# A hybrid S5 and pooling layer on one core: identity transposes at the start, the first projection ahead of the third tile, halves for the first loads, two queues for the last stores

## The chip, the cores and the metric

The kernel runs on one core of a Trainium2 chip (trn2). The metric is the device time of one execution in microseconds. TensorE is called PE here, VectorE DVE, ScalarE ACT, GpSimd POOL and SyncE SP.

## The reference, cut to what matters

One decoder layer: 2048 prompt tokens and 8 sample tokens, 1024 wide, all in float32.

```python
proj = h @ w_in                                  # (2048 + 8, 1024) @ (1024, 2048)
s_in, s_gate, p_in, p_gate = split(proj)         # four parts, 512 wide
sy, hr, hi = s5_mixer(s_in, ...)                 # 32 groups of 16 channels, complex state of 64, scan over time
sy = gelu(sy); sy = sy * sigmoid(sy @ glu_w + glu_b)
py, buf = pool_mixer(p_in, ...)                  # trailing means over 2, 4, 8, 16 tokens, a map per group
mixed = concatenate([sy * silu(s_gate), py * silu(p_gate)])
y = layer_norm(DN_ALPHA * h + mixed @ w_out)
```

## The kernel before, in words

**Precision.** Products run in the fp32r format, with each operand split in a high part (ACT converts, line 155) and a low part (DVE or POOL subtracts, line 149). A product of two operands is three matmuls: high by high, and the two mixed ones. `split` (line 154) does one tile.

**Start.** `load_x(i)` (line 497) loads tile i of the input, 128 tokens by 1024 (512 KB), `put_x(i)` (line 513) transposes it in eight 128x128 steps on PE against the constant `ident` (tile name pt, line 146), and splits the result into xh and xl. There are 16 prompt tiles and one of 8 sample tokens. `load_w` and `split_w` (lines 173, 179) load and split a 128-column piece of w_in (tiles wst and w). `proj(m, c)` (line 195) multiplies piece m by a chunk c of tokens, 8 blocks of k by 3 split terms = 24 matmuls into a PSUM bank pj; the first two chunks have 256 columns, then 512. `u_tile` (line 524) copies pj to ue on ACT and stores it as u_d. The first four m are the input of the S5 mixer.

**Parameters.** Between these, `params` (line 221) makes the tables of the S5 mixer from lambda, log_dt, B and C: small operations on DVE, a few transposes on PE (ps_par, which read nat; ps_c), 16 small copies prv on ACT (line 346), bbar on DVE, and then, per pair of groups, products on POOL (bd, qp, qq), sp on DVE, and ps_ks on PE (lines 428 and 146). `tables` (line 460) makes rotation tables (tb) on DVE.

**Middle and end.** 16 pairs of groups go through the scan (`ssm_task`): the input ut is split into uh, PE multiplies (s, line 629), ACT copies to SP, DVE turns and scans, PE multiplies by the output maps (y, pm). Projections for the gates and the pooling branch fill PE in between, each with a weight split w on ACT and DVE. Then come the GLU, the output projection and the layer norm; `out_last` (line 1132) ends the last tile of 128 tokens in two column halves, each stored in two pieces by `ln_store` (line 1071).

**What sets the order.** PE, ACT, DVE and POOL run their instructions in the order in which the program issues them. A clock by hand sets this order: `Line` (line 46) holds a time `line.t`, which `proj` moves on by 3n/2400 for every three matmuls and `put_x` by 0.9, and a list of generator tasks with due times; a task gives its next due time with `yield`. `line.t = 0.0` is set at line 550, after the first tiles. SP's queue, which issues all DMAs, is ordered by a scheduler of the framework. The buffers of the input tiles (xst two, xw two halves) are reused every four tiles, and a DMA waits also for the earlier one whose semaphore it takes, of eight.

Of the kernel before, what the change touches and what calls it, by code (L numbers as in the profile page):

```python
# [17 lines left out]
P = 128  # L18
# [3 lines left out]
KT = 8  # L22
# [20 lines left out]
HL = ((0, 0), (0, 1), (1, 0))  # L43
# [58 lines left out]
def hybrid_step(  # L102
# [9 lines left out]
    xp, xs = x_prompt[0], x_sample.rearrange("b l d -> (b l) d")  # L112
    wi, wo = w_in[0], w_out[0]
    dma = nc.sync.dma_start
    V, S, G = nc.vector, nc.scalar, nc.gpsimd
    line = Line()
# [5 lines left out]
    wst = ctx.enter_context(tc.tile_pool(name="wstage", bufs=1))  # L122
# [5 lines left out]
    def bank(name):  # L128
        return mm.tile([P, 512], F32, tag="bank", name=name)

    def pair(name):
        return pr.tile([P, 2, 512], F32, tag="pair", name=name)
# [12 lines left out]
    def transpose(out, in_, n):  # L145
        nc.tensor.transpose(out, in_, ident[:n, :n])
# [4 lines left out]
    def sub_hi(src, hi, lo, eng=None):  # L151
        tt(lo, src, hi.bitcast(F32), ALU.subtract, eng)

    def split(src, hi, lo, eng=None):
        S.copy(out=hi, in_=src)  # L155
        sub_hi(src, hi, lo, eng)
# [10 lines left out]
    def xcols(a, k, t0, n):  # L167
        h = t0 // 1024
        return xT[a][h][:, k, t0 - 1024 * h:t0 - 1024 * h + n]

    wtiles, wpend, ready, shared = {}, {}, {}, {}

    def load_w(src, key, pool=None, tag="wst"):
        st = (pool or wst).tile([P, KT * P], F32, tag=tag, name=f"wst_{key}")
        k = src.shape[0] // P
        dma(out=st.rearrange("p (k c) -> p k c", k=k), in_=src.rearrange("(k p) c -> p k c", p=P))
        return st

    def split_w(st, key, eng=None):
        w = wpool.tile([P, 2, KT * P], F32R, tag="w", name=f"w_{key}")  # L180
        split(st, w[:, 0], w[:, 1], eng)
        wtiles[key] = w

    def w_task(src, key, delay=4.0):
# [6 lines left out]
    def w_in_task(m, delay=6.4):  # L191
        wpend[m] = w_task(wi[:, P * m:P * m + P], m, delay)
        return wpend[m]

    def proj(m, c):
        t0, n, s = c
        n += s
        if m in wpend:
            line.finish(wpend.pop(m))
        ps = bank(f"pj{m}_{t0}")  # L200
        w = wtiles[m].rearrange("p a (k c) -> p a k c", k=KT)
        if m < 2:
            order = [(k, a, b) for a, b in ((0, 0), (1, 0), (0, 1)) for k in range(KT)]
        else:
            order = [(k, 0, b) for k in range(KT) for b in range(2)] + [(k, 1, 0) for k in range(KT)]
        for i, (k, a, b) in enumerate(order):
            nc.tensor.matmul(out=ps[:, :n], lhsT=w[:, a, k], rhs=xcols(b, k, t0, n), start=(i == 0), stop=(i == 23))  # L207
            if i % 3 == 2:
                line.go(3 * n / 2400.0)
        return ps  # L210

    ident = const.tile([P, P], F32, name="ident")
# [247 lines left out]
    def tables():  # L460
        while "table" not in ready or "x" not in ready:
            yield 0.5
        zs = shared["zs"]
        for q in range(4):
            tb = tabs[0].tile([P, 2, 4, HC], F32, tag="tb", name=f"tb{q}")
            V.memset(tb[:, 0, :, 0:1], 1.0)
            V.memset(tb[:, 1, :, 0:1], 0.0)
            for lv in range(6):
                n = 2 ** lv
                mt = tabs[0].tile([P, 2, 2, 128], F32, tag="mt", name="mt")  # L470
                mv = [mt[:, i, :, :4 * n].rearrange("p a (g c) -> p a g c", g=4) for i in range(2)]
                cmul(tb[:, :, :, n:2 * n], tb[:, :, :, 0:n],
                     [zs[:, c, 1 + lv, 4 * q:4 * q + 4].unsqueeze(1).unsqueeze(3) for c in range(2)],
                     mv[0], mv[1], [P, 2, 4, n])
                yield (1.12, 0.8, 0.8, 1.0, 1.4, 2.2)[lv]
            for a in range(2):
                dma(out=tb_d[4 * q:4 * q + 4, :, a].rearrange("g p c -> p g c"), in_=tb[:, a])
            yield 7.0
# [18 lines left out]
    def load_x(i):  # L497
        if i == 2:
            xstage["w"] = wpool.tile([P, 2, D], F32, tag="w", name="xw")
        if i % 4 > 1:  # L500
            st = xstage["w"][:, i % 2]
        else:
            st = xst.tile([P, D], F32, tag="x", name=f"xst{i}")
        if i == 0:
            for h in range(2):
                dma(out=st[:, 512 * h:512 * h + 512], in_=xp[0:P, 512 * h:512 * h + 512])
        elif i < 16:
            dma(out=st, in_=xp[P * i:P * i + P, :])
        else:
            dma(out=st[:NB], in_=xs)  # L510
        xstage[i] = st

    def put_x(i):
        st, n = xstage.pop(i), P if i < 16 else NB
        ps = pair(f"pt{i}")
        pv = ps.rearrange("p a b -> p (a b)").rearrange("p (k t) -> p k t", k=KT)
        for k in range(KT):
            transpose(pv[:, k, :n], st[:n, P * k:P * k + P], n)
        line.t += 0.9
        h, c = (i // 8, P * (i % 8)) if i < 16 else (1, 1024)  # L520
        hi, lo = (xT[a][h][:, :, c:c + n] for a in range(2))
        split(pv[:, :, :n], hi, lo)

    def u_tile(m, c):
        t0, n, s = c
        ps = proj(m, c)
        k0, nk = t0 // T, n // T
        ue = ga.tile([P, T, 64], F32, tag="g", name=f"ue{m}_{t0}")
        uv = ue.rearrange("p j k -> p (j k)")[:, :n].rearrange("p (j k) -> p j k", j=T)
        S.copy(out=uv, in_=ps[:, :n].rearrange("p (k j) -> p j k", j=T))  # L530
        dma(out=u_d[:, P * m:P * m + P, k0:k0 + nk].rearrange("j c k -> c j k"), in_=uv)
        if s:
            S.copy(out=us[:, m], in_=ps[:, n:n + s])

    PD = 0.5
    load_x(0)
    load_x(1)
    st0 = load_w(wi[:, 0:P], 0)
    load_x(2)
    load_x(3)  # L540
    st1 = load_w(wi[:, P:2 * P], 1, prod, "hl")
    put_x(0)
    load_x(4)
    split_w(st0, 0)
    put_x(1)
    load_x(5)
    put_x(2)
    load_x(6)
    split_w(st1, 1, G)
    line.t = 0.0  # L550
    par = line.add(params(ptmp, prod), PD)
    tab = line.add(tables(), 10.0)

    def x_task():
        for i in range(3, 17):
            put_x(i)
            if i + 4 < 17:
                load_x(i + 4)
            done.append(i)
            yield 2.88  # L560
        rx.close()
        with tc.using_default_side("right"):
            tabs.append(rx.enter_context(tc.tile_pool(name="tabs", bufs=1)))
        ready["x"] = True

    done = [2]
    xg = line.add(x_task(), 0.38)

    def need_x(i):
        while not done or done[-1] < i:  # L570
            for x in line.tasks:
                if x[1] is xg:
                    line.step(x)
                    break

    for c in CHUNKS_U:
        last = min(16, (c[0] + c[1] + P - 1) // P - 1) if not c[2] else 16
        if last > 1:
            need_x(last)
        for m in range(2):  # L580
            u_tile(m, c)
        if c[0] == 512:
            line.add(w_in_task(2))
# [484 lines left out]
    def ln_shift(mv, n):  # L1068
        V.scalar_tensor_tensor(out=mv[:n, 0:1], in0=mv[:n, 0:1], scalar=-1.0, in1=mv[:n, 2:3], op0=ALU.mult, op1=ALU.mult)  # L1069

    def ln_store(yout, ot, n, c):
        for j in range(len(yout)):
            dma(out=yout[j][:, c], in_=ot[j * n // len(yout):(j + 1) * n // len(yout), c])

    def ln_tail(xt, st, n, yout, nm):
        mv = ln_scale(st, n, nm)
# [55 lines left out]
    def out_last(mix, c0, xin, yout, nm):  # L1132
        xt = out_load(xin, P, nm)
        st = xo.tile([P, 3, 6], F32, tag="ste", name="ste", bufs=1)
        for i, (h, c) in enumerate(((0, full), (1, slice(0, 256)), (1, slice(256, 512)))):
            ps = po.tile([P, 512], F32, tag="o", name=f"o{nm}_{i}")
            out_mm(ps[:, c], lambda a, k: mix[:, a, k, c0:c0 + P], h, c, HL)
            ln_part(xt, ps[:, c], st[:, i], P, slice(512 * h + c.start, 512 * h + c.stop))
        mv = ln_scale(st, P, nm)
        cs = [slice(512 * h, 512 * h + 512) for h in range(2)]  # L1140
        for c in cs:
            V.scalar_tensor_tensor(out=xt[:, c], in0=xt[:, c], scalar=mv[:, 0:1], in1=gb[:, 0, c], op0=ALU.subtract, op1=ALU.mult)
        for c in cs:
            V.scalar_tensor_tensor(out=xt[:, c], in0=xt[:, c], scalar=mv[:, 2:3], in1=gb[:, 1, c], op0=ALU.mult, op1=ALU.add)
            ln_store(yout, xt, P, c)

    xpv = xp.rearrange("(k j) d -> j k d", j=T)
    ypv = y_prompt[0].rearrange("(k j) d -> j k d", j=T)
# [17 lines left out]
    for ck, (t0, n, s) in enumerate(CHUNKS[i] for i in BO):  # L1166
# [10 lines left out]
        for i in range(nt):  # L1177
            xin, yout = ([v[j, k0:k0 + nk, :] for j in range(nj * i, nj * i + nj)] for v in (xpv, ypv))
# [42 lines left out]
```

## Time and profile before

| what | value |
|---|---|
| three timed runs | 713.64, 714.81 (median), 717.47 us |
| the profiled execution, its own time | 712.72 us |
| span of the profile | 710.9 us |
| mean granted clock of TensorE | 0.987 |
| busy: PE, DVE, ACT, POOL | 96%, 70%, 33%, 27% of the span |

The span runs from the first instruction to the last; the execution's own time is 1.8 us longer. PE's busy time counts a matmul from its start to a modelled end, so 96% busy is not 96% of what PE could do.

### The profile page before, as it was taken

Reading aid. Unit: us, or ns where it says so; the run is one execution under the profiler, and the core shown is the slowest. Engines: PE = TensorE matmul, PEld = TensorE weight load, DVE = VectorE, ACT = ScalarE, POOL = GpSimd, SP = SyncE. Lnnn points to the kernel's source line nnn. Section 1 sums busy time; section 2 is a strip of 40 time slices with the busy share of each in tenths; the row PEclk is TensorE's granted clock in tenths of the full one; section 3 lists DMA queues with packets and bytes.
Section 4 is the critical chain, followed back from the end, with each engine's and each line's share of the span. In section 5 each row is a group of like instructions: output and inputs, shape, how many; then the busy total and the mean of one; then the engine's idle time right before and its main releaser. Section 6 shows DMA issues by size and latency. Waiting matters only on the chain.

```text
span 710.9 us, 10871 instructions
## 1 busy us (share of the span) xinstructions
PE 682.5 (96%) x3735; PEld 578.5 (81%) x3735; DVE 497.5 (70%) x1129; ACT 232.7 (33%) x471; POOL 195.5 (27%) x250
## 2 busy tenths in 40 slices
PE   6999899999999999999998999989999999999995
PEld 5988787888888888888977887777888868888884
DVE  3689889652679798888988893686555647647444
ACT  4343223331344344443332332353321332323100
POOL 1005444400000121232133213664314333062222
PEclk9999999999999999999998999999999999999998
DMA  8993578666555443443434326945454662633432
GB/s 275 226 336 112 141 208 204 190 211 184 161 164 160 131 138 110 141 123 101 138 116 122 94 90 140 356 131 114 115 117 124 142 155 62 148 105 103 118 90 59
DMA packets 133686, 105.86 MB, mean 149 GB/s; under 512 B 70211, under 2 KB 111335, under 8 KB 133623
## 3 DMA queue, kind: packets, MB, share of 16 engines
q1 hardware_dynamic: 133631, 105.17, 52.5%
q8 instruction: 29, 0.48, 0.3%
q14 instruction: 26, 0.21, 0.1%
HBM read 63.69 MB, written 41.68 MB: 148 GB/s over the span
## 4 chain that ended last, share of the span: by engine, by line
PE 63%; DVE 12%; ACT 3%; POOL 2%; DMA 2%; issue 2%; SPq 1%; DVEq 0%; ACTq 0%; POOLq 0%
PE pj L207 28%; PE o L1090 24%; PE z L1050 5%; POOL ws L149 2%; DVE SP L149 2%; DVE B L718 1%; PE y L644 1%; PE s L629 1%; PE os L1090 1%; PE y L702 1%; ACT SP L682 1%; PE pm L854 1%; DVE B L149 1%; DVE ini L714 1%; DVE w L149 1%
## 5 line engine op out<-in xcount | busy, mean ns | idle before, releaser
L207 PE MATMUL pj<-xh,w 128*128 128x512 f32 (+2 forms) x1312 | 336.1, 349 | 0.0
L207 PEld LDWEIGHTS pj<-xh,w 128*128 128x128 f32 x1312 | 226.0, 191 | 30.0
L207 PE MATMUL pj<-xl,w 128*128 128x512 f32 (+2 forms) x656 | 207.3, 348 | 0.0
L1090 PE MATMUL o<-wo,mix 128*128 128x512 f32 (+1 forms) x792 | 176.1, 383 | 0.8 <-ACT mix L155 0.8
L1090 PEld LDWEIGHTS o<-wo,mix 128*128 128x128 f32 x792 | 145.2, 188 | 30.7 <-ACT mix L155 1.1
L207 PEld LDWEIGHTS pj<-xl,w 128*128 128x128 f32 x656 | 120.3, 190 | 14.9
L149 POOL TENSOR_TENSOR xr<-xr,gb 128x1024 f32<-128x1024 f32 x15 | 36.0, 2398 | 48.4 <-DVE xr L149 43.1
L688 POOL COPY bus<-SP 128x16 f32<-128x16 f32 x16 | 9.3, 582 | 137.6 <-ACT SP L682 137.6
L1050 PE MATMUL z<-yh,w_g 128*128 128x512 f32 (+2 forms) x240 | 47.0, 356 | 0.0
L149 POOL TENSOR_TENSOR ws<-pc 128x527 f32<-128x527 f32 (+1 forms) x20 | 21.9, 1096 | 91.0 <-ACT pc L805 39.6
L1050 PEld LDWEIGHTS z<-yh,w_g 128*128 128x128 f32 x240 | 39.9, 193 | 6.7
L1079 ACT ACTIVATE xr<-xr,mv 128x1024 f32<-128x1024 f32 x15 | 18.7, 1244 | 79.4 <-DVE mv L1069 79.4
L1058 DVE SCALAR_TENSOR_TENSOR xr<-xr,o 128x512 f32<-128x512 f32 (+1 forms) x33 | 22.0, 667 | 26.1 <-PE o L1090 26.1
L149 POOL TENSOR_TENSOR ws<-ws 128x525 f32<-128x525 f32 (+5 forms) x30 | 37.6, 1252 | 3.3 <-DVE dh L149 1.1
L149 DVE TENSOR_TENSOR xl<-pt,xh 128x1024 fp32r<-128x1024 f32 (+1 forms) x17 | 19.8, 1164 | 17.4 <-ACT xh L155 17.3
L149 POOL TENSOR_TENSOR mv<-mv,mhalf 128x1 f32<-128x1 f32 x16 | 9.9, 618 | 74.5 <-DVE mv L1064 74.5
L718 DVE TENSOR_TENSOR_SCAN B<-r,ini,SP 128x64 f32<-128x64 f32 x96 | 29.8, 354 | 0.0
L149 DVE TENSOR_TENSOR yh<-y,yh 128x512 fp32r<-128x512 f32 (+2 forms) x20 | 12.2, 610 | 21.7 <-ACT yh L155 21.7
L149 DVE TENSOR_TENSOR mix<-y,mix 128x512 fp32r<-128x512 f32 (+2 forms) x20 | 18.3, 914 | 12.0 <-ACT mix L155 12.0
L155 ACT CAST hh<-hf 128x528 fp32r<-128x528 f32 x16 | 10.1, 633 | 50.2 <-DVE hf L149 47.3
L149 DVE TENSOR_TENSOR xr<-xr,gb 128x1024 f32<-128x1024 f32 x15 | 18.3, 1220 | 10.5 <-ACT xr L1079 10.5
L682 ACT COPY SP<-s 64x264 f32<-64x264 f32 x64 | 23.8, 372 | 3.8 <-PE s L629 3.2
(218 smaller groups left out, 881.1 us busy)
## 6 DMA issues: line engine op xcount, KB each, us to landing
wst<-in_w_in_dram SPq DMA_DIRECT2D x16, 512.0 KB
xr<-in_x_prompt_dram SPq DMA_DIRECT2D x24, 256.0 KB
out_dram<-xr SPq DMA_DIRECT2D x22, 256.0 KB
xw<-in_x_prompt_dram SPq DMA_DIRECT2D x8, 512.0 KB
wt_d<-wzero SPq DMA_DIRECT2D x4, 1024.0 KB
sw_d<-sv SPq DMA_DIRECT2D x8, 512.0 KB
qw_d<-qh SPq DMA_DIRECT2D x16, 256.0 KB
ws<-sw_d SPq DMA_DIRECT2D x16, 256.0 KB
```

Of the source, the lines that this page charges most:

```text
L149: (eng or V).tensor_tensor(out=out, in0=a, in1=b, op=op)
L155: S.copy(out=hi, in_=src)
L207: nc.tensor.matmul(out=ps[:, :n], lhsT=w[:, a, k], rhs=xcols(b, k, t0, n), start=(i == 0), stop=(i == 23))
L629: nc.tensor.matmul(out=ps[:, c, 0:264], lhsT=ws[:, c, a], rhs=uh[:, b, c, 8:272], start=(i == 0), stop=(i == 2))
L644: nc.tensor.matmul(out=py[:, c, 0:264], lhsT=wq[cs, r, a], rhs=hh[cs, b, r], start=False, stop=(i == 5))
L682: S.copy(out=SP[64 * c:64 * c + 64, a], in_=ps[64 * a:64 * a + 64, c, 0:264])
L688: G.tensor_copy(out=bus[:, :, :, gp], in_=SP[:, :, 256:264])
L718: V.tensor_tensor_scan(out=B4[:, a, h], data0=dec, data1=A4[:, a, h], initial=ini[a], op0=ALU.mult, op1=ALU.add)
L1050: nc.tensor.matmul(out=ps[:, :n], lhsT=w[:, a, k, P * (m % 2):P * (m % 2) + P], rhs=yh[:, b, k, :n], start=(i == 0), stop=(i == 11))
L1058: V.scalar_tensor_tensor(out=xt[:n, c], in0=xt[:n, c], scalar=ALPHA, in1=ps, op0=ALU.mult, op1=ALU.add)
L1079: S.activation(out=xt[:n], in_=xt[:n], func=AF.Identity, scale=mv[:n, 2:3], bias=mv[:n, 0:1])
L1090: nc.tensor.matmul(out=ps, lhsT=lhs(a, k), rhs=wo_view(k)[:, b, 512 * h + c.start:512 * h + c.stop], start=(i == 0), stop=(i == len(hl) * ...
```

## The change

It has seven parts.

1. After the first loads are issued, `busy(12)` puts 12 transposes of the constant `ident` on PE; 8 more follow after tile 0 and 8 after tile 1. Nothing reads their result.
2. Tile 1 and weight 0 are loaded in two halves, as tile 0 was; tiles 0 and 1 and weight 0 are split in two halves.
3. Tile 2 is no longer transposed ahead of the first projection. It is the first step of the task that brings the other tiles, due at 0.8 and then 1.1 later; the next steps are 2.88 apart as before.
4. The first chunk's projections take the split terms in another order: high weight by high and low input, then the low weight.
5. The split of weight 1 stands just ahead of the second projection.
6. `line.t = 0.0` is set before tile 2's transposes and not after them.
7. In `out_last` the stores of the first column half go out on ACT's queue.

```diff
-    def load_w(src, key, pool=None, tag="wst"):
+    def load_w(src, key, pool=None, tag="wst", parts=1):
...
-        dma(out=st.rearrange("p (k c) -> p k c", k=k), in_=src.rearrange("(k p) c -> p k c", p=P))
+        kp = k // parts
+        for i in range(0, k, kp):
+            dma(out=st.rearrange("p (k c) -> p k c", k=k)[:, i:i + kp], in_=src[P * i:P * (i + kp)].rearrange("(k p) c -> p k c", p=P))
...
-        split(st, w[:, 0], w[:, 1], eng)
+        n = KT * P // parts
+        for i in range(0, KT * P, n):
+            split(st[:, i:i + n], w[:, 0, i:i + n], w[:, 1, i:i + n], eng)
...
-            order = [(k, a, b) for a, b in ((0, 0), (1, 0), (0, 1)) for k in range(KT)]
+            order = [(k, a, b) for a, b in (HL if t0 == 0 else ((0, 0), (1, 0), (0, 1))) for k in range(KT)]
...
-        if i == 0:
+        if i < 2:
             for h in range(2):
-                dma(out=st[:, 512 * h:512 * h + 512], in_=xp[0:P, 512 * h:512 * h + 512])
+                dma(out=st[:, 512 * h:512 * h + 512], in_=xp[P * i:P * i + P, 512 * h:512 * h + 512])
...
-        split(pv[:, :, :n], hi, lo)
+        if i < 2:
+            for k in range(0, KT, 4):
+                split(pv[:, k:k + 4, :n], hi[:, k:k + 4], lo[:, k:k + 4])
+        else:
+            split(pv[:, :, :n], hi, lo)
...
+    def busy(n):
+
+        ps = pair("busy")
+        for i in range(n):
+            transpose(ps[:, i % 2, 0:P], ident, P)
+
...
-    st0 = load_w(wi[:, 0:P], 0)
+    st0 = load_w(wi[:, 0:P], 0, parts=2)
...
+    busy(12)
     put_x(0)
     load_x(4)
-    split_w(st0, 0)
+    busy(8)
     put_x(1)
     load_x(5)
-    put_x(2)
-    load_x(6)
-    split_w(st1, 1, G)
+    busy(8)
+    split_w(st0, 0, parts=2)
     line.t = 0.0
...
-        for i in range(3, 17):
+        for i in range(2, 17):
...
-            yield 2.88
+            yield 2.88 if i > 2 else 1.1
...
-    done = [2]
-    xg = line.add(x_task(), 0.38)
+    done = [1]
+    xg = line.add(x_task(), 0.8)
...
         for m in range(2):
+            if m and c[0] == 0:
+                split_w(st1, 1, G)
             u_tile(m, c)
...
-    def ln_store(yout, ot, n, c):
+    def ln_store(yout, ot, n, c, q=dma):
         for j in range(len(yout)):
-            dma(out=yout[j][:, c], in_=ot[j * n // len(yout):(j + 1) * n // len(yout), c])
+            q(out=yout[j][:, c], in_=ot[j * n // len(yout):(j + 1) * n // len(yout), c])
...
-            ln_store(yout, xt, P, c)
+            ln_store(yout, xt, P, c, dma if c.start else S.dma_start)
```

The start of PE's program before (pt: transposes of a tile, pj: a projection; each row is one kind of instruction and its count):

```order
L146 MATMUL pt_127<-ident,xst_115 128x128 x8
L146 MATMUL pt_143<-ident,xst_118 128x128 x8
L146 MATMUL pt_156<-ident,xw 128x128 x8
L207 MATMUL pj_0_171<-xh_85,w_140 128x256 x6
L146 MATMUL pt_178<-ident,xw 128x128 x8
L207 MATMUL pj_0_171<-xh_85,w_140 128x256 x10
L207 MATMUL pj_0_171<-xl_87,w_140 128x256 x8
```

And with the change, up to the parameter transposes:

```order
L146 MATMUL busy<-ident 128x128 x12
L146 MATMUL pt_142<-ident,xst_115 128x128 x8
L146 MATMUL busy<-ident 128x128 x8
L146 MATMUL pt_166<-ident,xst_118 128x128 x8
L146 MATMUL busy<-ident 128x128 x8
L211 MATMUL pj_0_195<-xh_85,w_190 128x256 x8
L211 MATMUL pj_0_195<-xl_87,w_190 128x256
L146 MATMUL pt_215<-ident,xw 128x128 x8
...
L211 MATMUL pj_0_260<-xh_85,w_257 128x256 x6
L146 MATMUL pt_267<-ident,xst_155 128x128 x8
L211 MATMUL pj_0_260<-xh_85,w_257 128x256 x2
L211 MATMUL pj_0_260<-xl_87,w_257 128x256 x8
L211 MATMUL pj_0_260<-xh_85,w_257 128x256 x5
L146 MATMUL ps_par<-ident,nat 128x16 x3
```

Tile 2 (pt_215) has moved behind nine matmuls of the first projection, and the parameter transposes ps_par from behind tile 5 to inside the second projection, ahead of it.

ACT's program, the conversions of the first tiles and weights with the change (xh: a tile, w: a weight, ue: the copy of a projection):

```order
L155 CAST xh_85<-pt_142 128x4x128 x2
L155 CAST xh_85<-pt_166 128x4x128 x2
L155 CAST w_190<-wst_121 128x512 x2
L155 CAST xh_85<-pt_215 128x8x128
L155 CAST xh_85<-pt_230 128x8x128
L538 COPY ue_0_254<-pj_0_195 128x256
L155 CAST w_257<-wst_127 128x1024
```

Weight 1 (w_257) stands behind the copy ue of the first projection; before, it stood behind tile 2. Further on, at the last full tiles, ACT's program before and then with the change (xh_86 from pt_666, then from pt_745, is tile 15):

```order
L155 CAST xh_86<-pt_606 128x8x128
L329 COPY cc<-ps_c 64x256 x4
L155 CAST xh_86<-pt_666 128x8x128
L346 COPY prv_677<-pw 128x16 x8
L346 COPY prv_678<-pw 128x16 x8
L155 CAST w_726<-wst_594 128x1024
```

```order
L155 CAST xh_86<-pt_648 128x8x128
L333 COPY cc<-ps_c 64x256 x4
L350 COPY prv_705<-pw 128x16 x8
L350 COPY prv_706<-pw 128x16 x8
L155 CAST xh_86<-pt_745 128x8x128
L155 CAST w_756<-wst_622 128x1024
```

Tile 15 has moved from ahead of the 16 copies prv to behind them.

DVE's program in the middle, at the fourteenth of the 16 pairs of groups, before and then with the change (B and ini: the scan, dh: the pooling branch, w: the low part of a weight, uh: the low part of the next pair's input):

```order
L149 TENSOR_TENSOR dh_0_4322<-df_0_4318,dh_0_4322 128x512
L712 TENSOR_SCALAR ini_3_4328<-B_4228,z_96 128x2
L714 SCALAR_TENSOR_TENSOR ini_3_4328<-B_4228,z_96,ini_3_4328 128x1 x2
L718 SCALAR_TENSOR_TENSOR B_4228<-r_94,ini_3_4328,SP_4223 128x64 x2
L149 TENSOR_TENSOR w_4340<-wst_4247,w_4340 128x1024
L149 TENSOR_TENSOR uh_4356<-ut,uh_4356 128x544
L149 TENSOR_TENSOR SP_4223<-B_4228,tbl_4124 128x2x256
```

```order
L149 TENSOR_TENSOR dh_0_4370<-df_0_4366,dh_0_4370 128x512
L149 TENSOR_TENSOR uh_4376<-ut,uh_4376 128x544
L149 TENSOR_TENSOR SP_4256<-B_4261,tbl_4129 128x2x256
L149 TENSOR_TENSOR B_4261<-B_4261,tbl_4129 128x512
L149 TENSOR_TENSOR hf<-SP_4256,B_4261 128x256 x2
L149 TENSOR_TENSOR w_4400<-wst_4305,w_4400 128x1024
L149 TENSOR_TENSOR hh_4412<-hf,hh_4412 128x528
```

The weight's low part has moved from ahead of uh to behind hf.

## Rows read from the trace of the kernel before

**Rows 1.** The page: busy time of each engine, share of the span, instructions.
```profile
PE 682.5 (96%) x3735; PEld 578.5 (81%) x3735; DVE 497.5 (70%) x1129; ACT 232.7 (33%) x471; POOL 195.5 (27%) x250
```
**Rows 2.** PE's waits over the run: for whom, us in total, times, longest.
```profile
PE s L629 <- DVE uh L149: 3.6, 2, 2.8
PE ps_ks L146 <- DVE sp L149: 3.5, 2, 2.7
PE pm L854 <- ACT dh L155: 3.4, 3, 1.4
```
**Rows 3.** Timeline, PE at the head: start, duration, instruction, count [idle before].
```profile
7.87 1.97 PE L146 MATMUL pt<-ident,xst 128*128 128x128 f32 x8 [1.71 <-DMA xst<-in_x_prompt_dram]
...
11.02 1.94 PE L146 MATMUL pt<-ident,xw 128*128 128x128 f32 x8 [1.18 <-DMA xw<-in_x_prompt_dram]
...
12.61 1.63 PE L207 MATMUL pj<-xh,w 128*128 128x256 f32 x6
...
14.04 1.91 PE L146 MATMUL pt<-ident,xw 128*128 128x128 f32 x8
...
18.18 1.04 PE L146 MATMUL pt<-ident,xst 128*128 128x128 f32 x8
```
**Rows 4.** Timeline, PE from the third chunk's approach to its second tile.
```profile
23.25 1.70 PE L207 MATMUL pj<-xh,w 128*128 128x256 f32 x12
...
24.80 1.04 PE L146 MATMUL pt<-ident,xw 128*128 128x128 f32 x8
...
30.84 0.87 PE L207 MATMUL pj<-xh,w 128*128 128x512 f32 x3
...
31.54 1.04 PE L146 MATMUL pt<-ident,xst 128*128 128x128 f32 x8
```
**Rows 5.** Timeline, ACT and DVE at the head.
```profile
9.56 1.04 ACT L155 CAST w<-wst 128x1024 fp32r<-128x1024 f32 x1 [2.35 <-DMA wst<-in_w_in_dram]
...
20.16 0.38 ACT L530 COPY ue<-pj 128x256 f32<-128x256 f32 x1
...
21.45 0.20 DVE L242 COPY nat<-dt 16x128 f32<-16x128 f32 x1
```
**Rows 6.** Timeline, tile 15 and the first ps_ks.
```profile
55.87 2.04 ACT L346 COPY prv<-pw 128x16 f32<-128x16 f32 x16 [0.65 <-DVE pw L149]
55.88 1.22 DVE L149 TENSOR_TENSOR xl<-pt,xh 128x1024 fp32r<-128x1024 f32 x1
...
59.09 1.30 DVE L149 TENSOR_TENSOR bm<-bbar,q 128x512 f32<-128x512 f32 x2
...
73.88 1.19 PE L146 MATMUL ps_ks<-ident,sp 128*128 128x128 f32 x4 [2.67 <-DVE sp L149]
```
**Rows 7.** Timeline, DVE's kv and a later ps_ks on PE.
```profile
80.38 0.41 DVE L149 TENSOR_TENSOR kv<-kf,kv 32x256 fp32r<-32x256 f32 x1 [2.27 <-ACT kv L155]
...
110.31 0.92 PE L146 MATMUL ps_ks<-ident,sp 128*128 128x128 f32 x4 [0.79 <-DVE sp L149]
```
**Rows 8.** Timeline, the fourteenth pair of groups.
```profile
371.77 2.04 DVE L149 TENSOR_TENSOR w<-wst,w 128x1024 fp32r<-128x1024 f32 x1
...
373.73 1.58 DVE L149 TENSOR_TENSOR uh<-ut,uh 128x544 fp32r<-128x544 f32 x1
...
375.37 1.47 PE L629 MATMUL s<-uh,ws 128*128 128x264 f32 x5 [2.85 <-DVE uh L149]
```
**Rows 9.** Stretches: length, busy PE, PEld, DVE, ACT, POOL, then PEclk, DMA share, GB/s.
```profile
320.00:330.00 10.00, 9.24 (x45) 7.48 (x44) 9.00 (x25) 1.62 (x5) 2.13 (x2) 1.00 0.32 103
375.00:382.00 7.00, 6.63 (x19) 5.48 (x20) 5.34 (x9) 3.22 (x8) 1.55 (x3) 0.53 0.54 158
```
**Rows 10.** Timeline, the end: DVE's last operations and SP's last four stores.
```profile
705.17 1.41 DVE L1144 SCALAR_TENSOR_TENSOR xr<-xr,mv,gb 128x512 f32<-128x512 f32 x2
705.95 2.39 SPq L1073 DMA_DIRECT2D out_dram<-xr  x4
```
**Rows 11.** Timeline, SP: issue of the first two cn loads.
```profile
21.62 3.04 SPq L240 DMA_DIRECT2D cn<-in_ssm_c_re_dram  x2
```

More of the change, by code (lines that the diff above doesn't have):

```diff
@@ L171, in hybrid_step, with split_w @@
     wtiles, wpend, ready, shared = {}, {}, {}, {}
-    def load_w(src, key, pool=None, tag="wst"):
+    def load_w(src, key, pool=None, tag="wst", parts=1):
         st = (pool or wst).tile([P, KT * P], F32, tag=tag, name=f"wst_{key}")
         k = src.shape[0] // P
-        dma(out=st.rearrange("p (k c) -> p k c", k=k), in_=src.rearrange("(k p) c -> p k c", p=P))
+        kp = k // parts
+        for i in range(0, k, kp):
+            dma(out=st.rearrange("p (k c) -> p k c", k=k)[:, i:i + kp], in_=src[P * i:P * (i + kp)].rearrange("(k p) c -> p k c", p=P))
         return st
-    def split_w(st, key, eng=None):
+    def split_w(st, key, eng=None, parts=1):
         w = wpool.tile([P, 2, KT * P], F32R, tag="w", name=f"w_{key}")
-        split(st, w[:, 0], w[:, 1], eng)
+        n = KT * P // parts
+        for i in range(0, KT * P, n):
+            split(st[:, i:i + n], w[:, 0, i:i + n], w[:, 1, i:i + n], eng)
         wtiles[key] = w
```

## The prediction

> **What bounds the kernel now.** I read the page first, then the list of waits, then the timeline at the places that the diff touches. TensorE is busy for 96% of the span [rows 1], so a gain elsewhere counts only where PE waits. The list of waits says where that is: at the head, at one transposition behind DVE (ps_ks), and in the middle behind uh and dh [rows 2]. At the head PE waits for tile 0, for tile 1 (1.71 us before 7.87) and for tile 2 (1.18 us before 11.02). The 8 transposes at 7.87 and 11.02 take 1.97 and 1.94 us, at 18.18 they take 1.04 [rows 3]: the granted clock is printed as 1.00 for both, but the durations fit the lower level (1.2 GHz) and the full one (2.4 GHz). From 11.02 on it has no wait of half a microsecond until 71.2.
>
> **The head.** Now 28 identity transposes fill PE's waits from about 1.4 us on (12 by 0.243, from 1.94/8, end at 4.3; tile 0's transposes then start later and cost nothing, since tile 1 lands at 7.87 anyway). I take it that they bring the full rate by about 7 us. Then tile 1 is transposed at 7.9 to 8.4, ACT converts its second half by 9.0 and the first half of weight 0 by 9.7 (half of the 1.04 us of [rows 5]); the first product starts at 9.7 where it started at 12.61 behind tile 2. From [rows 4], 12 products take 1.55 us (24.80 - 23.25), 0.129 each, and the 48 products and two tiles from 23.25 to 30.84 take 7.59, so a tile's 8 transposes step PE by 0.7. So: 9 products to 10.9, tile 2 (landed 11.0) to 11.8, 3 products to 12.2, tile 3 (landed between 11.0 and 14.0; I take 12.6) to 13.4, 12 products to 14.9, last result 15.1.
>
> Here a new wait comes: the split of weight 1 now stands behind the copy ue on ACT (the order shows it), and ue needs the last product. 0.38 for ue and 1.04 for the conversion [rows 5] plus hand-overs: the second projection starts at 16.65, PE idle 1.5. POOL's low half (about 2.4, twice DVE's 1.22 for the size [rows 6], an estimate) is needed 2.9 us after that and is in time. A second wait follows: PE reaches the parameter transposes after 6 products, tile 4 and 15 products, at 20.1, but they need the copy nat, which DVE does behind tile 4's low half: from the start of tile 4's transposes to the end of nat it took 3.47 us (18.18 to 21.65, [rows 3, 5]), so 17.4 + 3.47 = 20.9. With 0.5 for those transposes (an estimate, five at about 0.1) and then 51 products and three tiles (7.59 + 0.4 + 0.7), the 512-column chunk starts at **30.1 instead of 30.84**: 0.7 gained of the 2.9 at the start.
>
> SP: three more DMA issues lie in front of the second weight, and since each queue slot waits for its last load, tiles 4 and 5 are issued behind weight 0 and tile 3, and tiles 6 and 7 behind bbar and three cn loads, two of which took 3.04 us to issue [rows 11]. That puts tiles 6 and 7 at some 19 us, and PE wants them at 24.7 and 27.6. I cost it at nothing; it hides behind the products in between, and is worth up to 1.5 us where those loads take over 5 us.
>
> **To 75 us.** The table of tiles is now three 512-column products later in PE's order: tile 8 comes at 30.1 + 6 x 0.233 = 31.5, where it came at 31.54 [rows 4]. So DVE gets each tile when it got it, and the 0.7 us is no gain to DVE, which is full from 43 us on and for which PE waits 2.67 us at 73.88 [rows 6]. One thing is worse. ACT now converts tile 15 behind the 16 small prv copies. DVE is done with pw at 55.87; the copies take 2.04, the conversion 1.0: 58.9. DVE has 2.0 us of q work ahead of it (57.10 to 59.09 in [rows 6]), now from 55.9 to 57.9, then waits 1.0 us for tile 15. All behind it is later by that, so PE resumes at 74.9 instead of 73.88. POOL's products come later too, by 1.0 and the weight split of 1.2 that DVE now does ahead of bbar; PE needs them just ahead of the same stall, where DVE is later still. And three products that PE had done ahead of the stall are now behind it, 0.4 us: **+1.4** in all, the head's gain swallowed by a longer stall. If the wait for tile 15 is hidden it is +0.4; if tiles 6 and 7 are late as well, up to +2.9.
>
> **To 115 us.** The u_d stores now leave SP ahead of the table stores that they waited behind, so ACT's ue and kv come earlier and DVE's 2.27 us wait for kv goes; the sp products also stand ahead of six table operations. DVE is then ahead, and the wait of 0.79 us at 110.31 goes [rows 7]: **-0.8** (between 0 and -0.8).
>
> **The middle.** Line time now holds 0.9 us more at the same product, so every later task stands some three products earlier in PE's order, and pieces on DVE trade places. One trade lies on a wait. Before, the split of a weight stood ahead of uh at the fourteenth group: w 2.04, uh 1.58, and PE waited 2.85 us for uh, right behind another 0.8 [rows 2, 8]. The clock then fell: granted 0.53 on the mean of 375 to 382, which loses 7 x 0.47 = 3.3 us of full-rate work; waits of up to 1.4 us [rows 2] left it at 1.00 in 320 to 330 [rows 9]. Now uh stands ahead of w. That can save the 2.0 of w and, with the idle time down from 3.7 to about 1.7, 3 of the slow stretch. But DVE's work is the same by the next group, and it is 90% busy there [rows 9]: part of it will be asked back. I take **-2.5**, half of 2.0 + 3.0; the ends are -6.7 (3.7 idle and 3.0) and +1.0 (a w's 2.0 us put in front of another wait, half hidden).
>
> **The end.** Four stores issue on SP in 2.39 us from 705.95, 0.6 each, and DVE is done at 706.58 [rows 10]. With the first two on ACT's queue, SP issues the last two from 706.6, so the last leaves at 707.2 rather than 707.75: 0.55 at most. By the Trainium skill (DMA: Bandwidth & Descriptors, Issuing engines are not separate DMA queues) queues share the same 16 DMA engines and a second one saves issue time alone. No run here shows two queues yet. By that the 0.55 would be all there is. I take **-0.3**, the middle between 0 (transfers bound it) and 0.55.
>
> **Sum.** +1.4 - 0.8 - 2.5 - 0.3 = -2.2. The profiled execution took 712.72 us, so 710.5 on its terms. The three timed runs are 713.64, 714.81 and 717.47: the median lies 2.1 above the profiled one, and of all four the middle is 714.2, 1.5 above. I put the forecast there: 710.5 + 1.5 = **712.0**.
>
> **Rivals.**
> A, much faster: uh's trade keeps all of its 5.0 and tile 15's wait is hidden: 0.4 - 0.8 - 5.0 - 0.3 = -5.7, 708.5. For it: the clock's fall hangs on one stall. Against: DVE's load.
> B, slower: **the identity transposes do not bring the full rate.** In favour: PE was transposing or multiplying without a pause from 11.02, and the 8 transposes at 14.04 still took 1.91 [rows 3]; before 12.61 it did nothing but transposes. Against: the pauses of 1.71 and 1.18 lay between them, and now there are none. Then all 28 and tiles 0 and 1 run at 0.243: 12 end at 4.3, tile 0 at 6.3, 8 more at 8.2, tile 1 at 10.2, 8 more at 12.1. The first product starts at 12.1, and some 4 us of the work behind it lies at half rate (as from 12.61 on before [rows 3]), 1.2 us more beyond what the waits for tiles 2 and 3 took: everything to 75 us is 3.6 us later. That gives -2.2 + 3.6 = +1.4, 715.6; and +3.9, 718.1, if the middle gives nothing. It decides at tile 1: transposes of 0.24 us there mean B. The Trainium skill (TensorE: Matmul & The Clock Gate, Part 4: PE-mode transpose) says that the full rate does not come on in transposes, which do not count as work in the same way. No row here has transposes alone for longer than 2 us, so the trace does not settle it.
> C, no effect: the head is swallowed by DVE as above and the uh stall comes back one group later: 1.4 - 0.8 - 0.3 = +0.3, 714.5. For it: the middle chain runs on DVE.
>
> **Chances.** Forecast 0.40, A 0.13, B 0.27, C 0.20. A measurement of this kernel tells about 0.5% from no change, 3.6 us. Faster by more: most of A and a tail of the forecast, 0.18. Slower by more: B without the middle's gain, and late tiles, 0.13. Within: 0.69. The range takes A's 708.5 and B up to 717.5.
>
> **What would show it.** Right: first product near 9.7 to 10.4; PE idle 1.5 us in front of the second projection and about 1 us at the parameter transposes; the 512-column chunk at about 30; the ps_ks stall over 4 us long and ending near 75; no wait at 110; uh of the fourteenth group ahead of w and no granted 0.50 behind it. Wrong: transposes of 0.24 us at tile 1 and a chunk that starts behind 32 (B), a clock fall elsewhere between 280 and 420 (C), or a ps_ks stall that ends by 74.

## The result and the profile after

The changed kernel takes **722.98 us** in the median of four runs (720.37 to 724.36), the kernel before 714.22 in four runs beside them. The ratio is 1.011, with a 95% interval from 1.0074 to 1.0147: slower by 1.1%. The forecast was faster, and its range went up to 717.5. The profiled execution took 722.16 us, its span is 720.4.

PE's busy line of the page, for [rows 1], and PE's waits for [rows 2] (for whom, us in total, times, longest):

```profile
PE 687.3 (95%) x3763; PEld 581.2 (81%) x3763; DVE 496.3 (69%) x1132; ACT 231.7 (32%) x474; POOL 189.8 (26%) x250
```

```profile
PE ps_ks L146 <- DVE sp L149: 9.3, 3, 4.8
PE pj L211 <- ACT w L155: 2.8, 2, 1.4
PE pm L870 <- ACT dh L155: 2.7, 2, 1.4
PE s L645 <- DVE uh L149: 2.3, 3, 1.4
PE pm L870 <- DVE dh L149: 2.2, 4, 1.5
PE y L660 <- DVE hh L149: 1.1, 2, 0.5
PE y L660 <- ACT hh L155: 0.8, 1, 0.8
```

PE's added work is 28 transposes. What grew is the wait for DVE's sp, from 3.5 us to 9.3, and it has a new longest case of 4.8 us. The waits for uh went down (from 3.6 us to 2.3), those for DVE's dh grew from 0.6 us to 2.2, and 1.9 us of waiting for hh came, where there was 0.2.

**Where the time went.** From PE's rows I counted the columns that PE has pushed through, without the identity transposes, and compared the moments at which both kernels have the same count behind them. This is my working from the timelines, and gives PE's lag against the kernel before (minus: ahead), read at the time of the kernel before in the first row:

| us in the kernel before | 30 | 65 | 80 | 100 | 120 | 180 | 280 | 440 | 520 | end |
|---|---|---|---|---|---|---|---|---|---|---|
| the change | -0.7 | -0.7 | +1.3 | +1.3 | +7.4 | +8.1 | +8.4 | +8.8 | +9.6 | +9.4 |

Two thirds of it arise in 20 us. The head, for [rows 3, 4]:

```profile
1.36 2.82 PE L146 MATMUL busy<-ident 128*128 128x128 f32 x12 [1.36 <-POOL ident masks.py:199]
3.97 1.24 PE L146 MATMUL pt<-ident,xst 128*128 128x128 f32 x8
5.05 1.04 PE L146 MATMUL busy<-ident 128*128 128x128 f32 x8
...
10.44 1.26 PE L211 MATMUL pj<-xh,w 128*128 128x256 f32 x8 [1.39 <-ACT w L155]
...
16.75 0.98 PE L211 MATMUL pj<-xh,w 128*128 128x256 f32 x6 [1.41 <-ACT w L155]
...
30.14 1.55 PE L211 MATMUL pj<-xh,w 128*128 128x512 f32 x6
```

Twelve transposes take 2.82 us at first, eight take 1.04 from 5.05 on: the full rate is there by 5 us in this execution, and the first products run at it. The chunk of 512 columns starts at 30.14, 0.7 us ahead of [rows 4].

The stretch that made the loss, first on SP (the kernel before, then the change; start, duration of the issue, count):

```profile
92.10 0.91 SPq L477 DMA_DIRECT2D tb_d<-tb  x2
...
96.24 5.09 SPq L456 DMA_DIRECT2D wt_d<-kv  x8
```

```profile
92.16 0.36 SPq L481 DMA_DIRECT2D tb_d<-tb  x1
...
95.70 4.39 SPq L460 DMA_DIRECT2D wt_d<-kv  x7
100.14 0.45 SPq L481 DMA_DIRECT2D tb_d<-tb  x1
```

Then DVE, PE and the clock in a stretch (length, busy PE, PEld, DVE, ACT, POOL, then PEclk, DMA share, GB/s), all of the change:

```profile
103.62 0.06 DVE L470 MEMSET tb<- 128x4 f32 x1 [5.82 <-DMA tb_d<-tb]
...
111.93 2.85 DVE L149 TENSOR_TENSOR sp<-bbar,prv 128x256 f32<-128x256 f32 x4
```

```profile
115.66 1.24 PE L146 MATMUL ps_ks<-ident,sp 128*128 128x128 f32 x4 [4.84 <-DVE sp L149]
```

```profile
115.00:120.00 5.00, 4.34 (x12) 3.52 (x13) 2.88 (x5) 1.78 (x3) 0.32 (x1) 0.50 0.12 46
```

The second decay table has two stores. They used to leave SP together at 92.10. Now the second one stands behind the eight stores of kv, seven of them in one run of 4.39 us, and is issued at 100.14. The table's tile tb has one buffer, so DVE can't begin the third table before that store has read it, and waits 5.82 us, until 103.62. Behind it on DVE stand sv, kv, qh and the third table, and behind those sp, for which PE waits 4.84 us where it waited 0.79 [rows 7]. Behind that wait the granted clock is 0.50, the lower level. Of the 6.1 us that are lost between 100 and 120, the longer wait is 4.05 and the low clock about 2 (an estimate: 4.34 us of work at half rate). (This ps_ks is the fourth that is transposed; the expectations below call it the fifth.)

### The profile page after: what moved, and what is told of

Read it like the earlier page. It is cut to its first block, busy times and chain, and to the rows that moved or that the text cites. A ratio compares the mean times of both kernels' runs of the same rounds, so it can differ in the third digit from the quotient of the medians.

```text
span 720.4 us, 10933 instructions
## 1 busy us (share of the span) xinstructions
PE 687.3 (95%) x3763; PEld 581.2 (81%) x3763; DVE 496.3 (69%) x1132; ACT 231.7 (32%) x474; POOL 189.8 (26%) x250
## 4 chain that ended last, share of the span: by engine, by line
PE 59%; DVE 23%; DMA 5%; ACT 5%; issue 4%; SPq 2%; POOL 2%; DVEq 0%; ACTq 0%; POOLq 0%
PE pj L211 24%; PE o L1106 24%; PE z L1066 5%; DVE SP L149 3%; DVE B L734 3%; PE pt L146 2%; DVE B L149 2%; DVE ini L730 1%; POOL ws L149 1%; DVE sp L149 1%; SPq L460 1%; DVE tb L149 1%; PE os L1106 1%; DVE mt L149 1%; DVE uh L149 1%
## 5 line engine op out<-in xcount | busy, mean ns | idle before, releaser
L149 POOL TENSOR_TENSOR ws<-ws 128x525 f32<-128x525 f32 (+5 forms) x30 | 35.1, 1168 | 3.3 <-DVE dh L149 1.1
L149 DVE TENSOR_TENSOR xl<-pt,xh 128x1024 fp32r<-128x1024 f32 (+2 forms) x19 | 20.1, 1058 | 19.5 <-ACT xh L155 19.5
L734 DVE TENSOR_TENSOR_SCAN B<-r,ini,SP 128x64 f32<-128x64 f32 x96 | 31.8, 373 | 0.0
L781 DVE SCALAR_TENSOR_TENSOR g<-g,pj 128x512 f32<-128x512 f32 (+1 forms) x20 | 11.5, 576 | 21.7 <-ACT g L780 16.8
```

The source lines that it names most:

```text
L149: (eng or V).tensor_tensor(out=out, in0=a, in1=b, op=op)
L734: V.tensor_tensor_scan(out=B4[:, a, h], data0=dec, data1=A4[:, a, h], initial=ini[a], op0=ALU.mult, op1=ALU.add)
L781: V.scalar_tensor_tensor(out=g[:, :n], in0=g[:, :n], scalar=1.0, in1=jm(ps[:, :n]), op0=ALU.add, op1=ALU.mult)
```

## The experiments

All ratios are against the kernel before on the same chip, in runs taken beside each. The first four tell the parts of the change apart.

**Two buffers for tb.**

```diff
-            tb = tabs[0].tile([P, 2, 4, HC], F32, tag="tb", name=f"tb{q}")
+            tb = tabs[0].tile([P, 2, 4, HC], F32, tag="tb", name=f"tb{q}", bufs=2)
```

> The change as it is, with two buffers for the decay table tb where there was one. Theory (SP's order: one store of the second table stands behind the eight stores of kv, and DVE waits for the one buffer): DVE's wait of 5.82 us ahead of the third table's memset goes, the wait of 4.84 us ahead of the fifth ps_ks falls under 1.5, the granted clock in 115 to 120 us goes back from 0.50 to 1.00, and the time falls by 5 to 6 us, to 716 to 718 (1.003 to 1.006 of the kernel before). Rival (the loss lies in the head or in the order of the whole middle): nothing of that moves the time, which stays at 721 to 724 (1.011).

Measured: 716.49 us, ratio 1.0035 (1.0016 to 1.0054). SP still issues the second store behind those of kv, at 101.42. DVE and PE:

```profile
98.86 0.06 DVE L470 MEMSET tb<- 128x4 f32 x1
...
110.42 1.43 DVE L149 TENSOR_TENSOR sp<-bbar,prv 128x256 f32<-128x256 f32 x4
```

```profile
112.36 0.88 PE L146 MATMUL ps_ks<-ident,sp 128*128 128x128 f32 x4 [0.43 <-DVE sp L149]
```

```profile
115.00:120.00 5.00, 5.00 (x24) 4.13 (x23) 4.06 (x12) 1.82 (x5) 1.66 (x4) 1.00 0.60 201
```

The memset waits for nothing, PE for 0.43 us, the clock stays up, and the loss falls from 8.8 us to 2.5 by the medians, from 1.1% to 0.35% by the ratios, with nothing else moved on PE, DVE, ACT or POOL. The cause of about two thirds of the loss is shown: one store's place in SP's order, held against DVE by a single buffer.

**The old order behind the head.** The planner's clock starts 0.9 us earlier, so that from the third tile on PE, DVE, ACT and POOL have the rows of the kernel before in its order.

```diff
-    line.t = 0.0
-    par = line.add(params(ptmp, prod), PD)
-    tab = line.add(tables(), 10.0)
+    line.t = -0.9
+    par = line.add(params(ptmp, prod), PD + 0.9)
+    tab = line.add(tables(), 10.9)
...
-            yield 2.88 if i > 2 else 1.1
+            yield 2.88 if i > 2 else 0.48
```

> The change as it is, with the planner's clock started 0.9 us earlier and the delays of the three tasks set so that PE, DVE, ACT and POOL get the rows of the kernel before, in its order, from the third tile on; the head and the last stores stay changed. Theory (the head gives its 0.7 us and all of the loss is in the order behind it): 712.5 to 714.0 (0.997 to 0.9995 of the kernel before), no wait over 1.5 us ahead of the fifth ps_ks. Rival (the head itself costs, by the second projection's wait or by the tiles that now load later): 719 or more.

Measured: 717.56 us, ratio 1.0044 (1.0025 to 1.0062), between both expectations. The wait in question is 0.77 us (at 113.19), as before the change, so that half holds. But the earlier tiles made a loss of their own at the head: ACT now converts tile 4 too ahead of the second weight's split.

```profile
18.45 1.85 PE L211 MATMUL pj<-xh,w 128*128 128x256 f32 x8 [2.32 <-ACT w L155]
```

PE waited 2.32 us, the eight products behind it ran at the lower clock (granted 0.69 in 18 to 20 us and 0.50 in 20 to 22; 1.85 us against 0.98 for six in the change), and the chunk of 512 columns started at 31.82. The head was 1.0 us late where the change is 0.7 early. So this run doesn't price the order alone; `e2_w1_early` below mends it.

**No identity transposes.** The three calls of `busy` are left out.

```diff
-    busy(12)
...
-    busy(8)
...
-    busy(8)
```

> The change without its 28 identity transposes, all other rows in the same order. Theory (they bring the full rate early): tile 0's and tile 1's transposes take 0.24 us each as in the kernel before, the first product still waits for the weights' split and starts within 0.5 us of 10.4, its first products are slow, and the time is 0.5 to 2.5 us longer than the change's, 723.5 to 725.5 (1.013 to 1.016). Rival (the transposes only occupy PE ahead of tile 0, and the rate comes on without them): within 0.4 us of the change, 722.6 to 723.4.

Measured: 720.98 us, ratio 1.010 (1.0078 to 1.0123), no worse than the change and below both expected times. At the head the theory is right:

```profile
3.56 3.09 PE L146 MATMUL pt<-ident,xst 128*128 128x128 f32 x12 [3.56 <-DMA xst<-in_x_prompt_dram]
...
10.62 2.08 PE L211 MATMUL pj<-xh,w 128*128 128x256 f32 x8 [2.54 <-ACT w L155]
```

Tiles and first products run at the lower rate and the 512-column chunk starts at 31.81 instead of 30.14. But the 1.7 us did not reach the end: the waits for sp, which end when DVE is done, took up the difference (2.91 and 0.49 us at 114 to 115 instead of 4.84).

**The last stores on two queues alone.** The kernel before with only this:

```diff
...
-            ln_store(yout, xt, P, c)
+            ln_store(yout, xt, P, c, dma if c.start else S.dma_start)
```

> The kernel before with nothing changed but the last tile's stores: the second half's four go out on ACT's queue. From the profile of the change, where last product to end took 8.25 us against 8.31: 714.1 to 714.7, no difference that shows (0.999 to 1.001). Rival (my forecast of -0.3 us for this part): 0.9996, which a timing could not tell from none; the profile would show 8.0 us from the last product to the end.

The expectation names the second half's four stores; the edit moves the two of the first half, of four in all.

Measured: 713.53 us, ratio 0.9998 (0.9982 to 1.0013): no difference in time. In its profile 7.99 us lie between the start of DVE's last read of an output product and the end, against 8.35 in the kernel before; in the change and nine more kernels with this tail it is 8.22 to 8.24, and 8.32 in two more without it. The gain is 0.1 us, once 0.36.

**Late tables.** The converse of the first run: the kernel before, with only the tables' pause longer, which puts one tb store behind those of kv.

```diff
-            yield 7.0
+            yield 7.5
```

> The kernel before with one number changed: the pause behind each table is 7.5 instead of 7.0 in the planner's microseconds, which puts one store of the second table behind the eight stores of kv on SP, as the change does, with head and tail as they were. Theory (that place in SP's order is enough): DVE waits 4 to 6 us ahead of the third table's memset near 103 us, the fifth ps_ks waits 3.5 to 5.5 us, and the time is 5 to 7 us longer, 719 to 721.5 (1.007 to 1.010 of the kernel before). Rival (it costs only together with the changed head): 713.5 to 715 (1.000 to 1.001).

Measured: 717.88 us, ratio 1.0044 (1.0026 to 1.0062). SP issues the second store at 100.89, DVE's memset waits 2.24 us and PE waits behind it:

```profile
100.89 0.45 SPq L477 DMA_DIRECT2D tb_d<-tb  x1
```

```profile
103.15 0.06 DVE L466 MEMSET tb<- 128x4 f32 x1 [2.24 <-DMA tb_d<-tb]
```

```profile
112.44 0.48 PE L146 MATMUL ps_ks<-ident,sp 128*128 128x128 f32 x1 [2.96 <-DVE sp L149]
```

The place in SP's order costs time without the new head: 3.4 us by the medians, less than the 5 to 7 expected and more than the rival allowed. DVE had sv to do ahead of the memset in this order, and only then waited. The longer pause also moved some of DVE's own rows, the tables' against sp and sv, so the 3.4 us are the price of both together.

**The identity transposes alone**, twelve and twice eight, in the kernel before.

```diff
+    busy(12)
     put_x(0)
...
+    busy(8)
     put_x(1)
...
+    busy(8)
     put_x(2)
```

> The kernel before with the 28 identity transposes alone, twelve ahead of tile 0 and eight each ahead of tiles 1 and 2. Theory: tile 1's and 2's transposes and the first products run at full rate, PE is 1.5 to 2.5 us ahead at 20 us, but the first ps_ks ends its wait when DVE is done, near 74 us as before, so that the lead is gone by 80 us: 713.5 to 715.0 (0.999 to 1.001). Rival (the lead reaches the end): 711.5 to 712.7 (0.997 to 0.998).

Measured: 715.23 us, ratio 1.0011 (0.9991 to 1.0031): nothing, though PE was 2.9 us ahead at 25 us and 2.2 at the chunk of 512 columns (28.65, behind a wait of 0.52 us). The place is another than expected. By my count of columns it is still 1.7 ahead at 80 us; 1.0 goes at the ps_ks of 109 us (waits of 1.39 and 0.49 for sp) and 2.2 between 370 and 500 us.

**The old order, with the second weight split early.**

```diff
     split_w(st0, 0, parts=2)
+    split_w(st1, 1, G)
...
-            if m and c[0] == 0:
-                split_w(st1, 1, G)
```

on top of the old order above.

> The change in the old order behind the head (as in e1_order_back), with the second weights' split ahead of the first projection again. Theory: the wait of 2.32 us ahead of the second projection and the low clock behind it go, the 512-column chunk starts at 28.5 to 30.0 us, and the first ps_ks takes that lead back, since its wait ends with DVE's sp at 74 to 76 us: 713.5 to 716.0 (0.999 to 1.003). Rival (what e1_order_back lost at the head is what it lost in all): 711.5 to 713.5.

Measured: 714.09 us, ratio 0.9983 (0.9966 to 1.0000). The chunk starts at 28.90. The lead of 1.9 us is 1.4 at 80 us and gone at 160 us, and this profiled execution (715.41) is 2.8 us behind at 520. The new head in the old order is worth at most 2.4 us by the interval, which ends at no change.

**sp ahead of the table rows.** `e2_w1_early` with two buffers for tb, and the tables begun later:

```diff
+        yield 6.0
         zs = shared["zs"]
         for q in range(4):
-            tb = tabs[0].tile([P, 2, 4, HC], F32, tag="tb", name=f"tb{q}")
+            tb = tabs[0].tile([P, 2, 4, HC], F32, tag="tb", name=f"tb{q}", bufs=2)
```

> e2_w1_early with two buffers for tb and the tables begun 6 us later in the planner's time, which puts the first sp ahead of the table's rows on DVE. Theory (the first ps_ks waits for the table rows that stand ahead of sp on DVE): its wait falls from 2.7 to 4.1 us to under 0.5, the clock stays at 1.00 from 70 to 85 us, the lead of the head is kept, and the time is 707.5 to 711.5 (0.991 to 0.996 of the kernel before). Rival (DVE is the bound there, so the wait only moves to a later ps_ks or to the first s): 713 or more.

Measured: **709.61 us, ratio 0.9926 (0.9903 to 0.9950)**. It beats both kernels. DVE has sp done at 64.2 us, and the first ps_ks has no wait, at the full clock, where the change waited 4.06 us and `e2_w1_early` 2.83 and 0.49:

```profile
62.67 1.60 DVE L149 TENSOR_TENSOR sp<-sp,sp 128x256 f32<-128x256 f32 x2
64.23 0.06 DVE L471 MEMSET tb<- 128x4 f32 x1
```

```profile
69.64 0.66 PE L146 MATMUL ps_ks<-ident,sp 128*128 128x128 f32 x4
```

```profile
70.00:75.00 5.00, 5.00 (x37) 4.73 (x36) 4.19 (x9) 1.17 (x4) 4.74 (x9) 1.00 0.55 148
```

PE is 6.1 us ahead at 80 us, 4.0 at 180, 3.4 at 440 and 1.8 at the end, against a profile of the kernel before (712.72) that lies 1.8 us under its median here; this profiled execution (710.77) lies 1.2 over its own. The medians are 4.9 us apart. What the order and what the second buffer did to this was not tried apart.

The last four kernels start from this one.

**uh ahead of the weight's split at the fourteenth group**, my step on the middle alone. `e3_w_later` is the same edit with 12.4.

```diff
-                line.add(w_in_task(9 + gi))
+                line.add(w_in_task(9 + gi, 9.4 if gi == 2 else 6.4))
```

> e2_sp_first with the weights' split of the fourteenth group behind uh and ahead of hh on DVE and ACT, where the change has it (one task's pause 9.4 instead of 6.4 in the planner's time); nothing else moves on PE, DVE, ACT or POOL. Theory (my step on the middle, alone): the waits of 0.86 and 2.85 us at the fourteenth group fall to about 0.4, the low clock behind them goes, hh takes up to 1.4 us of it back, and 2.0 to 3.5 us stay: 706.0 to 707.6 (0.988 to 0.990 of the kernel before). Rival (DVE is full there, and what one wait gives the waits of the next groups take, as in the profile of the change): 708.8 to 710.

> As e3_uh_first with the pause 12.4: the split stands behind hh and dh too, in stretches where DVE waited for ACT. Theory: hh is not late then, and 3 to 4.5 us are gained over e2_sp_first, 705.0 to 706.6. Rival (the products of the next weights or the next dh wait for it): 708 or more.

Measured: 709.36 us (0.9933, 0.9912 to 0.9954) and 710.18 us (0.9944, 0.9918 to 0.9969). Neither gains over `e2_sp_first`, and the wait did not even shrink. PE in `e2_sp_first`, where another wait of 0.86 us stands ahead, and then in the first of the two:

```profile
371.62 0.96 PE L645 MATMUL s<-uh,ws 128*128 128x264 f32 x5 [2.85 <-DVE uh L149]
```

```profile
372.56 1.47 PE L645 MATMUL s<-uh,ws 128*128 128x264 f32 x5 [3.54 <-DVE uh L149]
```

DVE and POOL of the first:

```profile
364.78 0.23 DVE L728 TENSOR_SCALAR ini<-B,z 128x2 f32<-128x2 f32 x1
365.05 0.35 DVE L730 SCALAR_TENSOR_TENSOR ini<-B,z,ini 128x1 f32<-128x1 f32 x2
365.31 0.59 DVE L734 TENSOR_TENSOR_SCAN B<-r,ini,SP 128x64 f32<-128x64 f32 x2
...
368.18 1.07 DVE L728 TENSOR_SCALAR ini<-B,z 128x2 f32<-128x2 f32 x1
369.29 1.22 DVE L730 SCALAR_TENSOR_TENSOR ini<-B,z,ini 128x1 f32<-128x1 f32 x2
370.43 1.45 DVE L734 TENSOR_TENSOR_SCAN B<-r,ini,SP 128x64 f32<-128x64 f32 x2
371.81 0.69 DVE L149 TENSOR_TENSOR uh<-ut,uh 128x544 fp32r<-128x544 f32 x1
```

```profile
368.16 1.06 POOL L149 TENSOR_TENSOR ws<-pc 128x527 f32<-128x527 f32 x1 [4.76 <-ACT pc L821]
369.31 2.19 POOL L149 TENSOR_TENSOR ws<-ws 128x525 f32<-128x525 f32 x2
```

The three small groups of DVE rows take 3.7 us from 368.18 on; 3 us earlier in the same trace, with POOL idle, the same three took 0.23, 0.35 and 0.59. While POOL's window sums ran, the rows that stood on DVE were stretched: the scan's rows in this kernel, w and uh in the one before ([rows 8]: 2.04 and 1.58, against 1.22 and 0.69 where POOL is idle; its sums run from 371.67 to 376.2). Hence my 2.0 us for "w ahead of uh" was not the price of w's place.

**uh ahead of the last scan too**, on top of `e3_uh_first`.

```diff
+                if h == 3 and gp == 12:
+                    ssm_uh(gp + 1)
...
-            if gp + 1 < GP:
+            if gp + 1 < GP and gp != 12:
                 ssm_uh(gp + 1)
```

> e3_uh_first with the fourteenth group's uh emitted ahead of the last scan of the group before, so that on DVE and ACT it stands ahead of the rows that run beside POOL's window sums. Theory (those sums stretch whatever DVE rows run beside them by some 2.6 us, and s waits because uh is behind these rows, not because the weights' split is): the wait of 3.54 us at the fourteenth s falls under 0.8, the granted clock of 374 to 380 us goes from 0.65 to 1.00, hh comes no later than it did, and the time is 705.0 to 707.4 (0.987 to 0.991 of the kernel before). Rival (DVE is full in that stretch, so that hh or dh waits take over what s gives): 708.6 to 710.

Measured: 709.56 us, ratio 0.9933 (0.9918 to 0.9948).

```profile
367.81 1.28 PE L645 MATMUL s<-uh,ws 128*128 128x264 f32 x6
...
374.77 0.51 PE L660 MATMUL y<-hh,wq 64*128 64x264 f32 x4 [2.21 <-ACT hh L155]
375.81 1.18 PE L660 MATMUL y<-hh,wq 64*128 64x264 f32 x8 [0.53 <-DVE hh L149]
```

The wait for uh is gone, and 2.21 and 0.53 us of waiting for hh stand 7 us later. The granted clock of 374 to 380 us is 0.72 after 0.65. The rival's time came true. Its reason fits: from 366 to 384 us DVE is busy 16.4 of 18 us both here and in `e3_uh_first`, and the order of its rows chose only which product waits.

**The best kernel without the identity transposes.**

```diff
-    busy(12)
...
-    busy(8)
...
-    busy(8)
```

> e2_sp_first without the 28 identity transposes. Theory (with the first ps_ks out of the way the head's lead reaches the end): 1.5 to 2.0 us longer, 711.0 to 711.8 (0.995 to 0.996 of the kernel before). Rival (the lead is lost later in any case, as in e2_ident_only): within 0.5 us of e2_sp_first, 709.1 to 710.1.

Measured: 709.72 us, ratio 0.9934 (0.9914 to 0.9954), 0.1 us from `e2_sp_first`. The rival again: the transposes are worth nothing to the time even here. Its first product starts at 9.99 and by 16 us it is level with `e2_sp_first`, where PE waits for conversions instead.

## Why the prediction was wrong

- **The head: right.** Forecast -0.7, measured -0.7. The second projection waited 1.41 us for the weight's split (forecast 1.5), the parameter transposes 0.47 for nat (0.8), the chunk started at 30.14 (30.1). The first product was later than forecast (10.44, not 9.7): ACT began the second half of tile 1 only at 9.29, behind 0.76 us of waiting for DVE's low part of the first half, which I had put at nothing. The waits further on absorbed that. Tiles 6 and 7 were issued at 17.88 and came in time. **Rival B fell**: the identity transposes do bring the full rate. The loss is larger than B's worst case (718.1) and has another cause.
- **To 75 us: the number right, in part by luck.** The lag at 80 us is +1.3, forecast +1.4, and DVE waited for tile 15 as I had said:

```profile
58.42 1.23 DVE L149 TENSOR_TENSOR xl<-pt,xh 128x1024 fp32r<-128x1024 f32 x1 [1.00 <-ACT xh L155]
```

  But DVE came there 0.5 us ahead of the kernel before, which I had ruled out: it was done with pw at 55.3 and not at 55.9. So PE resumed at 74.22 behind a wait of 4.06 us, 0.3 us later than before and not 1.0. The rest of the +1.3 came behind the stall: the products that had moved there ran at the lower level (six take 1.47 us, from 75.15 to 76.62), and the granted clock was still 0.63 in 78 to 80 us, where it was 1.00 before. I had priced three products at the full rate, 0.4 us. The two misses nearly cancel.
- **To 115 us: this step failed**, -0.8 forecast, +6.1 measured (from +1.3 to +7.4). I wrote that u_d's stores leave SP ahead of the table stores and that ACT's ue and kv come earlier. That is so: DVE's wait for kv went from 2.27 [rows 7] to 0.52 us. But I priced the queue only for who gains by leaving early. I did not ask who holds the buffer of the store that now leaves late. The same new order of SP put the second tb store behind seven of kv's, 4.39 us of issues, and DVE, with its rows in fixed order, waited 5.82 us for tb. SP's rows, compared one by one, would have shown it. Two buffers for tb took 6.3 us off by the medians beside each, and the same misplacement put 3.4 us on the kernel before. From 120 to 180 us another 0.7 came, which was not looked into.
- **The middle: failed too**, -2.5 forecast, +0.7 measured between 180 and 440 us. At the fourteenth group PE waits 0.43 us for uh instead of 2.85 [rows 8], and the granted clock is 1.00 in 380 to 390, as forecast. The rows that follow, of the change:

```profile
380.36 0.88 PE L645 MATMUL s<-uh,ws 128*128 128x264 f32 x5 [0.43 <-DVE uh L149]
385.55 0.51 PE L660 MATMUL y<-hh,wq 64*128 64x264 f32 x4 [0.84 <-ACT hh L155]
386.59 0.75 PE L660 MATMUL y<-hh,wq 64*128 64x264 f32 x8 [0.52 <-DVE hh L149]
398.11 0.88 PE L645 MATMUL s<-uh,ws 128*128 128x264 f32 x5 [1.42 <-DVE uh L149]
```

```profile
380.00:390.00 10.00, 8.27 (x47) 6.57 (x48) 9.86 (x14) 5.08 (x12) 4.75 (x5) 1.00 0.39 116
390.00:400.00 10.00, 8.58 (x41) 6.89 (x40) 9.75 (x24) 1.05 (x3) 3.18 (x3) 1.00 0.32 106
```

  DVE is busy 19.6 of these 20 us, and the waits came back as 0.84, 0.52 and 1.42, then 1.55 for dh at 426. I had halved the gain for this and should have taken all of it, as rival C did. `e4_uh_before_scan` shows that without the rest of the change: no wait for uh, two for hh, no time gained. The reason was wrong too. With w's place alone (`e3_uh_first`) the wait stays, at 3.54 us. In the change the last scan's rows had moved ahead of dh as well, so that uh (379.59) comes ahead of POOL's window sums (380.11); these then stretch the rows of SP, B and hf (1.55, 1.43 and 1.50 us), and hh is late. And one reading was wrong: "waits of up to 1.4 us [rows 2] left it at 1.00 in 320 to 330 [rows 9]". The wait there is 0.76 us; the one of 1.41 is at 471.91, and in 470 to 480 the granted clock is 0.83.
- **The end: mis-sized**, about -0.1 for -0.3. The Trainium skill (DMA: Bandwidth & Descriptors, Issuing engines are not separate DMA queues) says that issuing from a second engine saves only the time of issuing; the 0.1 us do not go against it.
- A further 0.8 us came between 440 and 520 us, where PE waits for ACT's dh. The waits themselves are shorter than before (2.7 us for 3.4 [rows 2]), but behind them the granted clock is 0.93, 0.90 and 0.83 in the tens from 460 to 490, where before only 470 to 480 was low (0.83). What moved this was not tried.

## What to carry to other kernels

When a change shifts a planner's clock, compare the order of the store queue row by row, and ask of every store that moved back which buffer it holds and which engine needs that buffer next. Here one more buffer gave most of the loss back. A wait for an engine that is over 90% busy in its stretch was not gained in three tries at reordering that engine's rows, and a lead at the head only counts if no later wait ends with another engine's schedule. What gained, together with the second buffer, was moving the late result (sp) ahead of work that nobody waited for yet.

## What the runs showed of the hardware

- Transposes alone brought the full rate: after 12 identity transposes in 2.82 us and tile 0's, eight took 1.04 us from 5.05 on, with no product run so far. (The granted clock is printed as 1.00 from the start; the rate is read from the durations.) In `e2_sp_first` tile 0's still took 1.92 and the next eight 1.71, and eight took 1.09 from 7.45 on, again ahead of any product. The Trainium skill (TensorE: Matmul & The Clock Gate, Part 4: PE-mode transpose) says that transposes in that mode don't engage the full rate; these fp32 transposes did. The trace names them MATMUL and does not show whether the mode was on.
- DVE rows of 0.23, 0.35 and 0.59 us took 1.07, 1.22 and 1.45 beside POOL's sums of 1.06 and 2.19 us. By the Trainium skill (SBUF — State Buffer, Who interferes with whom) a DVE row with two inputs in SBUF contends with a POOL row that reads SBUF, for a shared pair of ports that is an exclusive lock. The durations are in line with that: the first DVE group ends at 369.25, POOL's first sum at 369.22. That first group reads one tensor and a scalar, so the rule for two inputs does not plainly cover it. DVE's statistics of the layer norm, which read one operand, took 0.69 us beside POOL's rows and without them.
